# One core's hybrid decoder layer: state-space rooms laid out over attention's early heads, memory norm, constant rows and exp table first

## The chip, the cores and the metric

The kernel runs on one core of a Trainium2 chip. The metric is the device time of one execution in microseconds: the median of 3 runs before is 2584.89 us (2584.29 to 2587.09). The profile is of one execution; its span, from the first to the last instruction, is 2585.2 us.

The core has five engines that run side by side, each with a queue of its own that is worked off in order: TensorE (PE, matrix products; its weight loads are shown as PEld), VectorE (DVE), ScalarE (ACT), GpSimd (POOL) and SyncE (SP, which issues all DMAs of this kernel). On-chip memory (SBUF) has 128 partitions; rooms are told below in bytes of one partition. Products land in PSUM, 8 banks of 2 KB a partition.

## The reference

One layer over 1024 tokens of width 1024, in float32. Cut to what matters:

```
h = rms_norm(x, g_pre_mix)
q, k, v, z, xbc, dt_raw, ga, gs = split(h @ w_in)
o_att = stick_breaking_attention(q, k, v)          # 16 heads of 64, causal
o_ssm = ssd_branch(z, xbc, dt_raw, ...)            # 32 heads in 4 groups, chunks of 128
merged = sigmoid(ga) * (o_att @ w_br_att) + sigmoid(gs) * (o_ssm @ w_br_ssm)
x = x + rms_norm(merged @ w_mix_out, g_post_mix)
mem_n = rms_norm(mem, g_mem)                       # 256 memory tokens
x = x + rms_norm(cross_attention(rms_norm(x, g_pre_xa), mem_n, w_xq, w_xkv, w_xo), g_post_xa)
x = x + rms_norm(swiglu(rms_norm(x, g_pre_ffn), w_gu, w_down), g_post_ffn)
```

The output is compared in float32, so nearly every product is made of three: each operand is split into a high part, rounded to TensorE's faster format, and a low part (the difference), and high x high, high x low and low x high are added up.

## The kernel before

Stages follow each other: norm and v, z, the convolved part x|B|C and most gates (by a Winograd-like scheme with seven products for eight), then attention (from about 645 us), the state-space stage with the keys and values of the memory tokens (from 1091 us), the branch projections and the mix (from 1478 us), cross-attention (from 1661 us), and the feed-forward part.

**Order.** The code is written once, straight through. A scheduler then places the instructions on each engine's queue ahead of time, by a simulated timeline: earlier code has priority, but an instruction whose inputs and rooms are ready may go ahead of an earlier one that still waits. On the chip each queue is fixed. `behind(marks)` keeps instructions of an engine behind a given one on that engine; `issue_behind` does it for one instruction.

**Rooms.** Tiles live in pools. Left pools are stacked upward from the bottom of the memory, right pools downward from the top; a stage that closes its pools gives the place to the next. At the very bottom lie 16,384 bytes reserved as scratch for DMA descriptors that software writes. A tile laid over older tiles waits for the last reader of just those tiles (`reuse_waits="tile"`). Within a pool with several buffers of a tag, the program's layout gives out the lowest first, then the highest, then downward.

**Attention** (from L737) holds on the left the activations (hT, to byte 85,248; the second half of them, b22 and t1, is read by the last gate projections), and on the right, at the lower end, the pool `qk`: four rooms of 4,096 bytes each for the queries (qs, from 86,784), the high keys (kh, from 103,168) and the low keys (kl, from 119,552). Heads 12, 13, 14 and 15 have the first, fourth, third and second room of each; in order of time head 12 is done first, head 15 last. Above lie `wt` (wth and wtl, the turned attention weights, 135,936 to 152,320) and `beta` (n0, n1, the scans). For each head `scores` (L846) makes the score product (L858, L859), a sigmoid on ScalarE (L860) and a scan on VectorE (L861); `values` (L866) turns the result on PE (L875), copies it (L878), takes the difference (L879) and multiplies by v (L887, L888). The last four gate blocks (`gate_proj`, a sigmoid at L825) are strewn between the last heads as work for PE.

**The state-space stage** (from L948) opens with left pools over hT and qk and right pools `ots` and `w3` over beta, v and the projection weights. It first makes constants on GpSimd and VectorE: a triangle (`low`, L980), and the fixed part of the rows from which a chunk's decays are made (`colrows`, L993 and L994; `keyrows`, L996 and L997). `prep` (L1027) loads a chunk's rows, makes the decays by a product (L1048) and the exponent on ScalarE (L1049), and multiplies them (L1050). `states` and `outp` carry the state and make the output, `flip` turns it, `branch` projects it. Chunks of two ahead are prepared; 32 chunks in all.

Into this stage the memory tokens are woven. `memory(m)` (L1169) loads 128 token rows (L1171), takes the mean square on ScalarE (L1173), the root on GpSimd (`rstd_of`, L152 and L153), the norm on VectorE (L1174), turns them on PE (L1178) and stores high and low parts (L1180, L1181) in two 8 KB tiles of the pool `ots`. The gain g_mem is loaded into a weight room of `w3`. `mem_quanta` then makes keys and values from 16 weight blocks of 512 KB (load at L1194, split by L98 and L101), shared out evenly over the first eight steps of the chunk loop; from the second mark on each product is put behind the chunk's second-last marked product on PE's queue.

**Later rooms that the prediction speaks of:** `kT` (L1444), the keys for cross-attention, a right tile at 147,200 to 155,392; the gains `gx` (g_post_mix, g_pre_xa), a left pool at 146,688 to 154,880; the operand pool `opd` of the down projection, on the left from 118,016.

Of the kernel before, what the change touches and what calls it, by code (L numbers as in the profile page):

```python
# [34 lines left out]
def hybrid_block(ctx, tc, a, out, dbg=None):  # L35
# [213 lines left out]
    with ExitStack() as pa:  # L249
# [486 lines left out]
        with ExitStack() as p2:  # L736
# [14 lines left out]
            V.memset(mask, 0.0)  # L751
            G.affine_select(mask[:, S - P:], mask[:, S - P:], [[-1, P]], ALU.is_gt, 1.0, base=0, channel_multiplier=1)

            marks = []
            PIN = 8
            FQ = 1

# [88 lines left out]
            def scores(h, half, tb, ns_):  # L846
                def run():
                    hd = heads[h]
                    if half == 0 and tb == 0:
                        differences(h)  # L850
                    b = half * 4 + tb
                    L = (b + 1) * P
                    nt = mk(bp, [P, (half + 1) * HALF], F32, f"n{half}")
                    ns_.append(nt)
                    for s0 in range(0, L, HALF):
                        s1 = min(L, s0 + HALF)
                        ps = mk(psc, [P, HALF], F32, "sc")[:, :s1 - s0]
                        T.matmul(ps, hd["qs"][:, b * P:(b + 1) * P], hd["kh"][:, s0:s1], start=True, stop=False)  # L858
                        marks.append(T.matmul(ps, hd["qs"][:, b * P:(b + 1) * P], hd["kl"][:, s0:s1], start=False, stop=True))  # L859
                        A.activation(nt[:, s0:s1], ps, AF.Sigmoid, scale=-(HD ** -0.5))  # L860
# [68 lines left out]
            for m in range(NM):  # L929
                h, half = m // 2, m % 2  # L930
                hp, r = m // 4, m % 4
                s1 = [scores((m + 1) // 2, (m + 1) % 2, tb, ns_[m + 1]) for tb in range(4)] if m + 1 < NM else []
                if r == 3:
                    nxt = qk_quanta(hp + 2)
                dn = nxt[(r + 1) % 4]
                if m >= NM - 5:
                    n = -(-len(late) // (NM - m))
                    dn, late = late[:n], late[n:]
                interleave((values(h, half, ns_[m]), 0, 1), (s1, 0, 0.7), (dn, 0, 1))

    accp = pool(ctx, "a8", 4)
    acc_ = [mk(accp, [P, 2, S], F32, "a8") for _ in range(4)]
    acc = [acc_[f // 2][:, f % 2, :] for f in range(KT)]

# [1 line left out]
    p3b = ExitStack()  # L949
    with ExitStack() as p3:  # L950
        AHEAD = 2
        gb = pool(p3, "gbs", 2)
        sm = pool(p3, "smp", 2)
        t4 = pool(p3, "s4p", 3)
        t2 = pool(p3, "s2p", 9)
        ep = pool(p3, "exps", 1)
        wr = pool(p3, "wr3", 3)
        wp = pool(p3b, "w3", 2, side="right")
        ot = pool(p3b, "ots", 2, side="right")
        ps = pool(p3b, "ps3", 1, PSUM)  # L960
# [14 lines left out]

        NROW, HEADS, ONES, PAIRS, LARGE = 2, 32, 0, 64, 2.0 ** 127
        low = mk(ep, [P, P], F32, "low")
        G.memset(low, 1.0)  # L980
        G.affine_select(low, low, [[1, P]], ALU.is_ge, 0.0, base=0, channel_multiplier=-1)
        colrows = [mk(ep, [P, GH, P], F32R, f"colrows{i}") for i in range(NROW)]
        keyrows = [mk(ep, [P, HALF], F32R, f"keyrows{i}") for i in range(2)]
        before, within = mk(t4, [P, GH, P], F32, "s4"), mk(t4, [P, GH, P], F32, "s4")
        G.memset(before, 1.0)
# [95 lines left out]
        def outp(n):  # L1081
# [20 lines left out]
                    marks.append(ins)  # L1102
            V.tensor_tensor(y, y, pd, ALU.add)
            V.tensor_tensor(y, y, zs, ALU.mult)
            junk = mk(t2, [P, HALF], BF16, "junk", bufs=1)
            ms = mk(stats, [P, 1], F32, "ms")
            A.activation(junk, y, AF.Square, scale=float(HALF) ** -0.5, accum_out=ms)

# [19 lines left out]
        def halves():  # L1128

            return mk(wp, [P, 4, 2, HALF], F32R, "bw")  # L1130
# [28 lines left out]
                V.tensor_tensor(acc[f][:, sl], acc[f][:, sl], pb, ALU.add)  # L1159


        mh = mk(ot, [P, KT, ML], F32R, "oth")
        mlo = mk(ot, [P, KT, ML], F32R, "otl")
        gj = mk(wp, [P, 4, D], F32, "bw")
        gm, junk_m = gj[:, 0], gj[:, 1]
        nc.sync.dma_start(gm, a["g_mem"][0].partition_broadcast(P))
        marks = []

        def memory(m):  # L1169
            xt = mk(wr, [P, D], F32, "wraw")  # L1170
            nc.sync.dma_start(xt, a["mem"][0][m * P:(m + 1) * P, :])  # L1171
            ms = mk(stats, [P, 1], F32, "ms")
            A.activation(junk_m, xt, AF.Square, scale=D ** -0.5, accum_out=ms)  # L1173
            V.scalar_tensor_tensor(xt, xt, rstd_of(ms), gm, ALU.mult, ALU.mult)  # L1174
            for kh in range(2):
                pt = mk(ps, [P, 4, P], F32, "mm", bufs=2)
                for k in range(4):
                    T.transpose(pt[:, k, :], xt[:, (kh * 4 + k) * P:(kh * 4 + k + 1) * P], ident)  # L1178
                ks, cs = slice(kh * 4, kh * 4 + 4), slice(m * P, (m + 1) * P)
                A.activation(mh[:, ks, cs], pt, AF.Copy)  # L1180
                V.tensor_tensor(mlo[:, ks, cs], pt, mh[:, ks, cs].bitcast(F32), ALU.subtract)  # L1181

        def mem_quanta():

# [66 lines left out]

        for n in range(AHEAD):
            prep(n)
        for m in range(2):
            memory(m)
        mq = list(mem_quanta())
        NQ = len(mq)

# [610 lines left out]
```

## Time and profile before

| | us |
|---|---|
| median of 3 runs (lowest to highest) | 2584.89 (2584.29 to 2587.09) |
| span of the profiled execution (no other time is recorded for it) | 2585.2 |
| PE busy | 2493.1 |
| DVE busy | 1793.6 |
| ACT busy | 1130.1 |
| POOL busy | 842.2 |
| last score product of attention starts | 1070.20 |
| last product of attention's values starts | 1090.80 |
| products of the memory tokens, first starts | 1121.82 |

How to read it: the kernel's time is the span and a little around it. A busy PE includes the time that products take at a lower clock, so a window has to be read with the clock beside it (PEclk; 1.00 is full). A row of the timeline gives an instruction's start from the span's beginning, its length, and in brackets how long its engine stood idle before it and what released it. Products overlap: a 128x512 product at full clock is listed with 0.39 us, while the next one starts 0.23 us later.

### The profile page before, as it was taken

How to read it: one execution, taken by the hardware profiler on the slowest of the kernel's cores; microseconds unless marked ns; L12 is line 12 of the kernel's file. 1: busy time of each engine (PE TensorE's matmuls, PEld its weight loads, DVE VectorE, ACT ScalarE, POOL GpSimd, SP SyncE). 2: the span in 40 equal slices, each digit the busy share in tenths (PEclk: the TensorE clock that was granted, in tenths of full speed). 3: DMA queues.
4: the chain of work that ended last, by engine and by line, in shares of the span. 5: the costliest groups of instructions: out<-in, count | busy, mean ns of one | idle time of the engine just before them, and what ended most of it. 6: DMA issues, size and time to landing. Idle time of an engine off the chain costs nothing. (4 is left out here: it accounts for less than half of the span.)

```text
span 2585.2 us, 32334 instructions
## 1 busy us (share of the span) xinstructions
PE 2493.1 (96%) x11866; PEld 2061.1 (80%) x11866; DVE 1793.6 (69%) x2093; ACT 1130.1 (44%) x2020; POOL 842.2 (33%) x650
## 2 busy tenths in 40 slices
PE   7999999999999999999999999999999999999998
PEld 5788887887888778787888788887787888887876
DVE  7765777776578887687888664416459666666997
ACT  5333455555466655455554312314234333334343
POOL 3221654443111111244655050101114333323762
PEclk9999999999999999989999999999999999999999
DMA  7431433333543443355322462411232232224232
GB/s 245 155 121 58 151 117 103 109 106 91 141 107 98 118 104 90 111 180 175 104 90 81 153 238 74 130 49 50 94 113 70 76 96 74 90 90 163 98 131 98
DMA packets 255272, 293.44 MB, mean 114 GB/s; under 512 B 17024, under 2 KB 175241, under 8 KB 254987
## 3 DMA queue, kind: packets, MB, share of 16 engines
q1 hardware_dynamic: 255114, 291.40, 36.2%
q8 instruction: 93, 1.52, 0.2%
q14 instruction: 65, 0.52, 0.1%
HBM read 200.10 MB, written 74.45 MB: 106 GB/s over the span
## 5 line engine op out<-in xcount | busy, mean ns | idle before, releaser
L861 DVE TENSOR_TENSOR_SCAN n<-n,mask 128x128 f32<-128x128 f32 (+7 forms) x128 | 189.6, 1506 | 23.5 <-ACT n L860 22.2
L101 DVE TENSOR_TENSOR sw<-sf,sw 128x512 fp32r<-128x512 f32 x150 | 129.0, 872 | 67.0 <-ACT sw L98 66.7
L183 POOL TENSOR_TENSOR sf<-wr,wr 128x512 f32<-128x512 f32 x38 | 59.3, 1560 | 277.8 <-DMA wr<-in_w_gu_dram 138.3
L878 ACT ACTIVATE wth<-tr,mone 128x512 fp32r<-128x512 f32 x192 | 110.6, 584 | 83.0 <-PE tr L875 82.3
L98 ACT ACTIVATE sw<-sf 128x512 fp32r<-128x512 f32 x150 | 92.0, 626 | 109.1 <-PE mm L217 94.0
L879 DVE SCALAR_TENSOR_TENSOR wtl<-tr,wth 128x512 fp32r<-128x512 f32 x192 | 99.7, 544 | 50.6 <-ACT wth L878 50.6
L101 DVE TENSOR_TENSOR sw<-wr,sw 128x512 fp32r<-128x512 f32 x113 | 107.7, 955 | 27.6 <-ACT sw L98 27.5
L217 PE MATMUL mm<-h,sw 128*128 128x512 f32 x320 | 124.8, 391 | 1.8 <-DVE sw L101 1.8
L215 PE MATMUL mm<-h,sw 128*128 128x512 f32 x320 | 122.6, 391 | 2.9 <-ACT h L98 2.3
L216 PE MATMUL mm<-h,sw 128*128 128x512 f32 x320 | 125.1, 391 | 0.0
L104 PE MATMUL mm<-oth,bw 128*128 128x512 f32 (+1 forms) x320 | 122.5, 383 | 2.3 <-DVE a L1159 2.0
L98 ACT ACTIVATE sw<-wr 128x512 fp32r<-128x512 f32 x113 | 70.7, 628 | 120.9 <-PE mm L217 120.8
L106 PE MATMUL mm<-oth,bw 128*128 128x512 f32 (+1 forms) x320 | 120.0, 375 | 1.5 <-DVE bw L1146 1.5
L105 PE MATMUL mm<-otl,bw 128*128 128x512 f32 (+1 forms) x320 | 119.1, 372 | 0.0
L663 DVE SCALAR_TENSOR_TENSOR b<-b,prmT,b 128x1023 f32<-128x1023 f32 (+2 forms) x72 | 108.6, 1511 | 10.7 <-ACT b L661 10.0
L94 POOL TENSOR_SCALAR v<-va 128x512 fp32r<-128x512 f32 x16 | 20.6, 1291 | 285.4 <-PE av L888 165.8
L860 ACT ACTIVATE n<-sc 128x512 f32<-128x512 f32 (+1 forms) x192 | 88.6, 494 | 45.6 <-PE tr L875 28.8
L152 POOL TENSOR_SCALAR rstd<-ms 128x1 f32<-128x1 f32 x74 | 27.9, 376 | 242.3 <-ACT x L1380 111.5
L104 PE MATMUL p<-bw,h 128*128 128x512 f32 x256 | 99.4, 393 | 3.3 <-DVE x L1382 2.4
L106 PE MATMUL p<-bw,h 128*128 128x512 f32 x256 | 100.8, 394 | 0.0
L105 PE MATMUL p<-bw,h 128*128 128x512 f32 x256 | 100.4, 392 | 0.0
L185 POOL TENSOR_TENSOR sf<-wr 128x512 f32<-128x512 f32 x38 | 63.4, 1667 | 110.2 <-DVE sw L101 110.2
(607 smaller groups left out, 8033.1 us busy)
## 6 DMA issues: line engine op xcount, KB each, us to landing
wr<-in_w_gu_dram SPq DMA_DIRECT2D x80, 256.0 KB
wr<-in_w_in_dram SPq DMA_DIRECT2D x36, 512.0 KB
zr<-in_w_in_dram SPq DMA_DIRECT2D x28, 512.0 KB
gu_d<-t SPq DMA_DIRECT2D x44, 256.0 KB
wraw<-in_w_in_dram SPq DMA_DIRECT2D x20, 512.0 KB
zs_d<-zo SPq DMA_DIRECT2D x32, 256.0 KB
xs_d<-b SPq DMA_DIRECT2D x32, 256.0 KB
kl<-gt SPq DMA_DIRECT2D x64, 128.0 KB
```

The lines of the kernel that those rows point to most:

```text
L98: A.activation(o, i, AF.Copy)
L101: eng.tensor_tensor(o, i, hi.bitcast(F32), ALU.subtract)
L104: first = T.matmul(ps, sh, mh, start=start, stop=False)
L105: T.matmul(ps, sh, ml, start=False, stop=False)
L106: T.matmul(ps, sl, mh, start=False, stop=stop)
L215: T.matmul(ps, w[0][:, k, :], bh, start=first and k == 0, stop=False, skip_group_check=True)
L216: T.matmul(ps, w[0][:, k, :], bl, start=False, stop=False, skip_group_check=True)
L217: ins = T.matmul(ps, w[1][:, k, :], bh, start=False, stop=last and k == 3, skip_group_check=True)
L663: V.scalar_tensor_tensor(acc[:, sh:], y[:, :S - sh], cw(3 - sh, f), acc[:, sh:], ALU.mult, ALU.add)
L861: V.tensor_tensor_scan(nt[:, 0:L][:, ::-1], nt[:, 0:L][:, ::-1], mask[:, S - L:][:, ::-1], 1.0, ALU.mult, ALU.max)
L878: A.activation(wh[:, t0 * P:], pt[:, t0 * P:], AF.Identity, bias=mone)
L879: V.scalar_tensor_tensor(wl[:, t0 * P:], pt[:, t0 * P:], -1.0, wh[:, t0 * P:].bitcast(F32), ALU.add, ALU.subtract)
```

## The change

It touches the seam between attention and the state-space stage, and one line of the set-up.

- **Scratch.** The reserved bytes at the bottom go from 16,384 to 1,024. All left pools of the program sink by 15,360 bytes; right pools stay.
- **Exp table.** The sigmoids of the scores are collected (`sig`); behind the last one a one-column exp is put on ScalarE.
- **Memory tokens first.** `memory` is split in two: load and square (`memory_load`, both row tiles), then norm and turn (`memory`). Both stand ahead of the constants and of `prep` now, where before they stood behind `prep` of the first two chunks. The square's unused output goes into `mlo`; g_mem takes a raw room of the pool `wr3`.
- **Rooms.** The left pools of the stage are put in another order, and new ones are split off: `junk3` (the unused output of a chunk's square), `fill3` (512 bytes, never used), `memT` (mh and mlo, which were in `ots`) and `cols` (colrows; the pool `keys` keeps low and keyrows). A first weight room (`halves()`) and a first `dec` bank are taken and not used, so that those that follow come in the same turn as before.

| pool | before | after | what lay there in attention (after) |
|---|---|---|---|
| smp | 64,768 to 91,392 | 37,120 to 63,744 | activations (hT) |
| keys (low, keyrows) | in exps, 131,328 to 144,128 | 63,744 to 68,352 | activations |
| junk3, fill3 | in s2p; none | 68,352 to 69,888 | activations, to their end |
| memT (mh, mlo) | in ots, right | 69,888 to 86,272 | nothing |
| wr3 (raw blocks, token rows) | 144,128 to 156,416 | 86,272 to 98,560 | qs of heads 12, 15, 14 |
| s4p | 91,392 to 103,680 | 98,560 to 110,848 | qs of 14, 13; kh of 12, 15 |
| cols (colrows) | in exps | 110,848 to 119,040 | kh of 15, 14, 13 |
| s2p | 103,680 to 131,328 | 119,040 to 145,664 | kh of 13, kl, wth |
| gbs (states) | 52,480 to 64,768 | 145,664 to 157,952 | wtl, n0 |

The core of the diff:

```
-            marks = []
+            marks, sig = [], []
...
-                        A.activation(nt[:, s0:s1], ps, AF.Sigmoid, scale=-(HD ** -0.5))
+                        sig.append(A.activation(nt[:, s0:s1], ps, AF.Sigmoid, scale=-(HD ** -0.5)))
...
+            sig_last = sig[-1:]
...
+    with behind(sig_last):
+        A.activation(warm, mone, AF.Exp)
...
+        sm = pool(p3, "smp", 2)
+        ep = pool(p3, "keys", 1)
+        jk = pool(p3, "junk3", 1)
+        filler3 = pool(p3, "fill3", 1)
+        mk(filler3, [P, 128], F32, "fill3")
+        mtp = pool(p3, "memT", 1)
+        wr = pool(p3, "wr3", 3)
+        t4 = pool(p3, "s4p", 3)
+        cp3 = pool(p3, "cols", 1)
+        t2 = pool(p3, "s2p", 9)
         gb = pool(p3, "gbs", 2)
-        sm = pool(p3, "smp", 2)
-        t4 = pool(p3, "s4p", 3)
-        t2 = pool(p3, "s2p", 9)
-        ep = pool(p3, "exps", 1)
-        wr = pool(p3, "wr3", 3)
...
+        mh = mk(mtp, [P, KT, ML], F32R, "mh")
+        mlo = mk(mtp, [P, KT, ML], F32R, "mlo")
+        gm = mk(wr, [P, D], F32, "wraw")
+        nc.sync.dma_start(gm, a["g_mem"][0].partition_broadcast(P))
+        marks = []
+        mem_x = []
+        def memory_load(m):
+            xt = mk(wr, [P, D], F32, "wraw")
+            nc.sync.dma_start(xt, a["mem"][0][m * P:(m + 1) * P, :])
+            ms = mk(stats, [P, 1], F32, "ms")
+            A.activation(mlo.rearrange("p k t -> p (k t)")[:, m * D:(m + 1) * D], xt, AF.Square, scale=D ** -0.5, accum_out=ms)
+            mem_x.append((xt, rstd_of(ms)))
+        def memory(m):
+            xt, r = mem_x[m]
+            V.scalar_tensor_tensor(xt, xt, r, gm, ALU.mult, ALU.mult)
...
+        mk(ps, [P, 4, P], F32, "dec", bufs=2)
+        for fn in (memory_load, memory):
+            for m in range(2):
+                fn(m)
...
-        colrows = [mk(ep, [P, GH, P], F32R, f"colrows{i}") for i in range(NROW)]
+        colrows = [mk(cp3, [P, GH, P], F32R, f"colrows{i}") for i in range(NROW)]
...
-            junk = mk(t2, [P, HALF], BF16, "junk", bufs=1)
+            junk = mk(jk, [P, HALF], BF16, "junk")
...
-        mh = mk(ot, [P, KT, ML], F32R, "oth")
-        mlo = mk(ot, [P, KT, ML], F32R, "otl")
-        gj = mk(wp, [P, 4, D], F32, "bw")
-        gm, junk_m = gj[:, 0], gj[:, 1]
...
+        halves()
...
-        for m in range(2):
-            memory(m)
...
-    nc = _bacc.Bacc("TRN2", target_bir_lowering=False, num_devices=1)
+    nc = _bacc.Bacc("TRN2", target_bir_lowering=False, num_devices=1, dynamic_dma_scratch_size=1024)
```

More of the change, by code (lines that the diff above doesn't have):

```diff
@@ L970, in hybrid_block @@
         four = {}
+        mh = mk(mtp, [P, KT, ML], F32R, "mh")
[13 more added lines that the diff above has]
+            V.scalar_tensor_tensor(xt, xt, r, gm, ALU.mult, ALU.mult)
+            for kh in range(2):
+                pt = mk(ps, [P, 4, P], F32, "mm", bufs=2)
+                for k in range(4):
+                    T.transpose(pt[:, k, :], xt[:, (kh * 4 + k) * P:(kh * 4 + k + 1) * P], ident)
+                ks, cs = slice(kh * 4, kh * 4 + 4), slice(m * P, (m + 1) * P)
+                A.activation(mh[:, ks, cs], pt, AF.Copy)
+                V.tensor_tensor(mlo[:, ks, cs], pt, mh[:, ks, cs].bitcast(F32), ALU.subtract)
+        mk(ps, [P, 4, P], F32, "dec", bufs=2)
+        for fn in (memory_load, memory):
+            for m in range(2):
+                fn(m)
         NROW, HEADS, ONES, PAIRS, LARGE = 2, 32, 0, 64, 2.0 ** 127
@@ L1159, in branch @@
                 V.tensor_tensor(acc[f][:, sl], acc[f][:, sl], pb, ALU.add)
-        mh = mk(ot, [P, KT, ML], F32R, "oth")
-        mlo = mk(ot, [P, KT, ML], F32R, "otl")
-        gj = mk(wp, [P, 4, D], F32, "bw")
-        gm, junk_m = gj[:, 0], gj[:, 1]
[L1166 to L1181, printed above, removed]
+        halves()
         def mem_quanta():
```

## The prediction

> **What bounds the kernel now.** I read the cores first, then the busy tenths of the page, then the windows around the change.
>
> ```profile
> core 0: 2585.2 us, clock 0.990
> ...
> PE   7999999999999999999999999999999999999998
> ...
> DVE  7765777776578887687888664416459666666997
> ```
>
> One core works, and TensorE is busy in nearly every slice at full clock. So a change pays only where PE stands still, or runs at a lower clock, and later work can close up. The windows give the seam between attention and the state-space stage; columns are length, then busy time and count of PE, PEld, DVE, ACT and POOL, the granted clock, the DMA share and GB/s.
>
> ```profile
> 1051.00:1071.00 20.00, 20.00 (x101) 16.70 (x100) 9.70 (x12) 7.38 (x16) 0.00 (x0) 1.00 0.17 53
> 1071.00:1091.00 20.00, 17.89 (x100) 14.27 (x98) 12.25 (x18) 11.73 (x22) 11.03 (x12) 1.00 0.58 159
> 1091.00:1111.00 20.00, 15.18 (x68) 11.66 (x67) 19.47 (x23) 15.60 (x26) 11.13 (x9) 0.74 0.71 213
> 1111.00:1131.00 20.00, 16.99 (x93) 14.35 (x94) 18.26 (x23) 9.37 (x18) 7.62 (x9) 0.74 0.48 138
> 1131.00:1151.00 20.00, 20.00 (x169) 19.87 (x168) 12.22 (x14) 11.21 (x20) 7.20 (x7) 1.00 0.62 192
> ```
>
> From 1071 to 1131 PE loses 2.11 + 4.82 + 3.01 = 9.9 us idle, and (15.18 + 16.99) x 0.26 = 8.4 us to a clock of 0.74: 18.3 us, the ceiling of what this seam can return. Between 1091 and 1131 VectorE is the full engine (19.47 and 18.26 of 20), while it had 7.75 us free in the 20 us before. The timeline says why. These rows are start, length, engine, line, operation and, in brackets, idle time before and its releaser:
>
> ```profile
> 1070.20 0.39 PE L859 MATMUL sc<-kl,qs 128*128 128x512 f32 x1
> ...
> 1090.66 1.28 DVE L993 CAST colrows<-s 128x1024 fp32r<-128x1024 f32 x2
> ...
> 1090.80 0.33 PE L888 MATMUL av<-wtl,v 128*128 128x128 f32 x1
> ...
> 1091.60 0.38 SPq L1171 DMA_DIRECT2D wraw<-in_mem_dram  x1
> ...
> 1097.22 1.06 ACT L1173 ACTIVATE bw<-wraw 128x1024 f32<-128x1024 f32 x1 [0.28 <-DMA wraw<-in_mem_dram]
> 1098.19 0.19 ACT L1173 ACTIVATION_READ_ACCUMULATOR bw<-wraw 128x1 f32 x1
> ...
> 1098.39 0.43 SPq L1194 DMA_DIRECT2D wraw<-in_w_xkv_dram  x1
> ...
> 1098.77 1.30 POOL L153 TENSOR_TENSOR rstd<-rstd,mhalf 128x1 f32<-128x1 f32 x1
> ...
> 1103.71 1.05 ACT L98 ACTIVATE bw<-wraw 128x1024 fp32r<-128x1024 f32 x1
> ...
> 1120.67 1.27 DVE L1181 TENSOR_TENSOR otl<-mm,oth 128x512 fp32r<-128x512 f32 x2
> ...
> 1121.82 0.41 PE L104 MATMUL mm<-oth,bw 128*128 128x256 f32 x1
> ```
>
> The work that could fill PE, the products of the memory tokens, starts at 1121.82, right behind the last half of the turned tokens (otl). Its chain begins at 1091.60 with the load of the first token rows, because their room lies over attention's weight tiles (wtl), whose last reader is the product at 1090.80. The cast of the constant rows at 1090.66 stands behind the same rooms. Attention's last score product read its query and key rooms already at 1070.20.
>
> **The change part by part.** *Smaller scratch.* Left rooms sink by 15,360 bytes, right ones stay. Nothing is added, and no transfer needs the scratch: all data went by one hardware queue, and every issue row is SyncE's. Cost taken: nothing; its bound upward is a rival below.
>
> ```profile
> q1 hardware_dynamic: 255114, 291.40, 36.2%
> ```
>
> *Token rows, constant rows and their rooms.* The turned tokens (mh, mlo, 16 KB) now lie between the end of attention's activations and its lowest query room, free all through attention. The gain g_mem takes the lowest raw room, over head 12's queries, free long before. The two row tiles take the highest and the middle room; both touch head 15's queries (90,880 to 94,976, the higher one by 512 bytes), so they still wait for 1070.20. Their two loads pass ahead of the state-space loads on SyncE and move from 1091.60 to about 1071, 20 us. From there I use the same durations: 5.6 us to the square (1091.60 to 1097.22), 1.25 for it, 1.7 to GpSimd's end at 1100.07, 1.9 on VectorE (3.8 for two, below), 8 turns of PE, then copies and differences; the second tile two to three us behind. The last half stands at about 1087 instead of 1121.9. The first weight block has to wait, new in this version, for one of the three raw rooms (before, g_mem lay elsewhere): about 1083, plus 5.3 us (1098.39 to 1103.71), plus the split, 1.05 on ScalarE and 1.56 on VectorE (below): 1091. So the fill can begin about when attention ends, 30 us earlier.
>
> That is not 30 us of time, since VectorE is the full engine there. What leaves its full stretch is in the grouped lines (busy us, mean ns), all but the first of these rows, which is the difference of a weight block:
>
> ```profile
> L101 DVE TENSOR_TENSOR bw<-wraw,bw 128x1024 fp32r<-128x1024 f32 x4 | 6.2, 1561 | 1.7 <-ACT bw L98 1.7
> ...
> L1174 DVE SCALAR_TENSOR_TENSOR wraw<-wraw,rstd,bw 128x1024 f32<-128x1024 f32 x2 | 3.8, 1876 | 0.5 <-POOL rstd L153 0.5
> ...
> L1181 DVE TENSOR_TENSOR otl<-mm,oth 128x512 fp32r<-128x512 f32 x4 | 2.5, 676 | 0.0
> L994 DVE TENSOR_TENSOR colrows<-ident 16x1024 fp32r<-16x1024 f32 x2 | 2.3, 1211 | 0.0
> ...
> L993 DVE CAST colrows<-s 128x1024 fp32r<-128x1024 f32 x2 | 1.3, 683 | 0.0
> L997 DVE TENSOR_SCALAR keyrows<-low 2x512 fp32r<-2x512 f32 x2 | 0.8, 411 | 0.0
> L996 DVE CAST keyrows<-s 128x512 fp32r<-128x512 f32 x2 | 0.8, 419 | 0.0
> ```
>
> They are 11.5 us. The stretch 1071 to 1091 has 20 - 12.25 = 7.75 free, so 7.75 us are hidden there and 3.75 stay. The term lies between 0 (no step of the chain moves with it) and -18.3 (the ceiling); I take **-7.75**, since VectorE, being full, is the row nearest to the bound.
>
> *ScalarE.* To the same 20 us come two squares (2 x 1.25), four copies and the table work. The early exp is queued behind the last score sigmoid, which starts at 1070.63. But gate sigmoids follow; the first row below, of another view, has the copies (min, median and max ns):
>
> ```profile
> L1180 ACT ACTIVATE oth<-mm x4: 578/589/598, 1104.7 to 1113.8; 128x512 fp32r<-128x512 f32 x4
> ```
>
> ```profile
> 1070.63 0.60 ACT L860 ACTIVATE n<-sc 128x512 f32<-128x512 f32 x1 [1.67 <-PE sc L859]
> ...
> 1074.80 1.09 ACT L825 ACTIVATE gt<-mm 128x512 f32<-128x512 f32 x2 [1.19 <-PE mm L106]
> ...
> 1083.60 0.60 ACT L825 ACTIVATE gt<-mm 128x512 f32<-128x512 f32 x1 [0.24 <-PE mm L106]
> ...
> 1087.80 0.63 ACT L98 ACTIVATE ch<-cfm 128x512 fp32r<-128x512 f32 x1 [1.94 <-DMA cfm<-cf_d]
> ...
> 1098.39 1.28 ACT L1049 ACT_TABLE_LOAD   x1
> 1099.68 1.09 ACT L1049 ACTIVATE s<-dec 128x512 f32<-128x512 f32 x2
> ```
>
> So I expect three table loads where there is one: exp near 1071, sigmoid before 1074.80, exp again at the first chunk's exponent. The load that stood before the first exponent still stands there; two are added, 2 x 1.28 = 2.6 us. Together 2.5 + 2.4 + 2.6 = 7.5, against 20 - 11.73 = 8.3 free: hidden, barely. What is queued behind them is attention's weight copies (L878), for which DVE and then PE wait; without cover the cost is 2.6. I take 0. The Trainium skill, "ScalarE: Activation LUTs", section "What ACT_TABLE_LOAD costs", gives 1283 ns for the load and 1380 ns of drain at every switch. The trace agrees with the load; here the next activation starts 0.01 us after it, so no drain is to be seen. By the Trainium skill the two switches would be 5.3 us, which would not fit, and the sum would be 2.7 us higher.
>
> *Rooms elsewhere.* kT lay over the gain g_pre_xa, whose last reader is the VectorE instruction at 1668.15; in the new layout that gain is 15,360 bytes lower and kT's room is free.
>
> ```profile
> 1668.15 1.28 DVE L161 SCALAR_TENSOR_TENSOR x<-x,rstd,g_pre_xa 128x1024 f32<-128x1024 f32 x1 [0.98 <-POOL rstd L153]
> ...
> 1674.60 0.67 PE L1472 MATMUL p<-kT,qT 128*128 128x256 f32 x2 [0.67 <-DMA kT<-kT_d]
> ...
> 2357.27 0.50 PE L1645 MATMUL dnb<-op,op 128*128 128x512 f32 x1 [1.42 <-ACT op L98]
> ```
>
> PE waited 0.67 us for that load: **-0.67**. The start of the down projection (1.42 us of wait) also gets other rooms under its operands; it may lose this wait or get a like one: 0, bounds 1.42 both ways. The first attention-branch weights no longer wait for the square's scratch (its own room now), but PE has other products there: 0.
>
> Sum: -7.75 - 0.67 = -8.4; 2585.2 - 8.4 = 2576.8. The profiled span is 0.3 us over the median of the runs (2584.9), so 2576.5.
>
> **The rivals.**
>
> *The clock comes back too.* If PE has products from 1091 on, its clock need not fall, and part of the 8.4 us is saved on top: about 2568. For it speaks that the clock is 1.00 in all windows in which PE is full; against it that VectorE stays nearly full. The Trainium skill, "TensorE: Matmul & The Clock Gate", Part 1, says that the clock halves after an idle window of some 3.4 us and returns after as long a busy one. By that rule the 0.74 is a consequence of the gaps and goes with them.
>
> *The fill is spent, not added.* The memory products are a fixed supply, and each is queued behind a chunk's products. If the chunk steps do not move, the supply ends earlier than its last row now, and PE meets earlier what it meets in these windows:
>
> ```profile
> L104 PE MATMUL mm<-bw,oth x32: 388/393/507, 1151.7 to 1185.1; 128*128 128x512 f32 x32
> ...
> 1171.00:1191.00 20.00, 19.51 (x107) 16.24 (x106) 14.96 (x18) 11.02 (x20) 7.05 (x6) 1.00 0.62 192
> 1191.00:1211.00 20.00, 17.02 (x90) 13.64 (x89) 17.18 (x19) 13.41 (x26) 10.29 (x10) 1.00 0.64 220
> ```
>
> Without fill PE lost 2.98 us of 20 against 0.49 with it. Then most of the 7.75 is given back, some 1.5 us remain: 2583. Against it: the constant rows move too, and with them the first chunks.
>
> *Slower: ScalarE blocks attention's tail.* Its queue is in order. In the row at 1087.80 it stood 1.94 us for a load, with attention's copies behind it. Now the squares of both row tiles, loaded only from 1071 on, stand in that queue, each up to 5.6 us behind its load: 11.3 us at worst, and the two table loads 2.6: 13.9. Against the 8.4 gained that is +5.5: 2590.4. It decides from 8.4 us of such waits on. Against it: the loads overlap, and gate products keep PE busy until 1083.
>
> *It does not do what it says:* the exp table does not come first, which is in the sum already; and if the small scratch did bind transfers after all, DMA shares of 0.6 to 0.7 in the seam would rise and all stages would lose, which I give no more than 2 in 100, within the slower case.
>
> **How the numbers follow.** Forecast (2572 to 2579) 0.46, clock too 0.13, fill spent 0.24, slower 0.17. A measurement of this kernel tells about 0.2% (5.2 us) from no change: faster 0.46 + 0.13 = 0.59, the same 0.24, slower 0.17. The range goes from 2585 - 18.3 = 2567 to the slower case with one more wait of 1.42: 2592.
>
> **What would show it.** Right: token loads near 1071, last mlo near 1087, first memory product near 1091, constant rows cast before 1085; three table loads between 1070 and 1100; a clock above 0.74 in 1091 to 1131, and VectorE fuller before 1091. Wrong: ScalarE idle before a square with attention's copies late; attention's last product well after 1091; gaps after the memory products as long as those saved; a transition elsewhere (270, 645, 1480, 1960, 2357 us) shifted by more than 2 us.

## The result, and the profile after

The changed kernel took 2576.03 us (median of 4 runs, 2572.78 to 2577.68); the kernel before, beside it, 2585.02 (2584.29 to 2587.09). The ratio is 0.9961 with a 95% interval of 0.9949 to 0.9973: 7 to 13 us faster, against 8.4 forecast. The profiled span fell from 2585.2 to 2575.9. The total hides that one term was too large and two too small, so the stages come first.

Page and windows after; the columns of a window are length, busy time and count of PE, PEld, DVE, ACT and POOL, granted clock, DMA share and GB/s:

```profile
core 0: 2575.9 us, clock 0.993
...
1071.00:1091.00 20.00, 16.20 (x85) 12.25 (x84) 15.82 (x23) 13.56 (x25) 8.51 (x8) 0.98 0.56 182
1091.00:1111.00 20.00, 19.02 (x122) 17.39 (x123) 17.76 (x19) 14.49 (x25) 10.42 (x7) 0.85 0.71 225
1111.00:1131.00 20.00, 18.68 (x134) 16.79 (x133) 16.67 (x19) 9.82 (x17) 9.21 (x8) 1.00 0.61 173
1131.00:1151.00 20.00, 17.45 (x112) 15.02 (x111) 17.57 (x18) 13.12 (x24) 13.65 (x12) 1.00 0.66 207
1151.00:1171.00 20.00, 18.97 (x102) 15.92 (x101) 17.03 (x20) 12.42 (x22) 9.67 (x9) 1.00 0.56 186
1171.00:1191.00 20.00, 18.09 (x101) 15.03 (x99) 14.95 (x16) 11.74 (x21) 8.41 (x8) 1.00 0.61 205
1191.00:1211.00 20.00, 17.55 (x98) 14.32 (x97) 17.83 (x22) 11.90 (x24) 10.47 (x10) 1.00 0.44 134
1211.00:1231.00 20.00, 17.91 (x91) 15.30 (x90) 16.29 (x18) 9.55 (x21) 12.87 (x12) 0.91 0.34 95
```

Two windows of the kernel before that the prediction did not need:

```profile
1151.00:1171.00 20.00, 19.11 (x99) 15.54 (x97) 15.47 (x15) 10.87 (x19) 8.06 (x7) 1.00 0.54 185
1211.00:1231.00 20.00, 18.69 (x107) 16.07 (x106) 13.95 (x19) 11.30 (x22) 12.31 (x13) 1.00 0.29 88
```

Multiply PE's busy time by the clock to get its work. From 1091 to 1131 it was (15.18 + 16.99) x 0.74 = 23.8 us before and 19.02 x 0.85 + 18.68 = 34.8 after: 11.0 more, half of it filled idle time (5.5), half the clock. But from 1131 to 1231 the five windows fall from 94.3 to 88.4 (the last one at a clock of 0.91), 6.0 less, and from 1071 to 1091 from 17.9 to 15.9, 2.0 less. So some 3 us remain of 11, and another 0.9 comes after 1231. The gain stands where the change was made; what it cost stands in the windows on both sides.

Where PE stands can be read from first and last starts. The rows hold name, count, shortest, median and longest duration in ns, and the first and last start. Before:

```profile
L859 PE MATMUL sc<-kl,qs x192: 220/364/479, 670.8 to 1070.2; 128*128 128x512 f32 x96, 128*128 128x128 f32 x32, 128*128 128x256 f32 x32, 128*128 128x384 f32 x32
...
L888 PE MATMUL av<-wtl,v x192: 221/423/486, 685.7 to 1090.8; 128*128 128x512 f32 x96, 128*128 128x384 f32 x32, 128*128 128x256 f32 x32, 128*128 128x128 f32 x32
...
L105 PE MATMUL pst<-s2r,bh x28: 389/389/795, 1092.1 to 1413.0; 128*128 128x512 f32 x28
...
L104 PE MATMUL mm<-oh,whi x128: 389/389/500, 1478.3 to 1566.9; 128*128 128x512 f32 x128
...
L1472 PE MATMUL p<-kT,qT x128: 377/379/483, 1674.6 to 1785.5; 128*128 128x256 f32 x128
L1444 SPq DMA_DIRECT2D kT<-kT_d x1: 326/326/326, 1669.5 to 1669.5; - x1
...
L1645 PE MATMUL dnb<-fw,fg x24: 389/389/389, 2350.2 to 2369.2; 128*128 128x512 f32 x24
L1645 PE MATMUL dnb<-op,op x24: 389/389/504, 2357.3 to 2372.9; 128*128 128x512 f32 x24
```

And after:

```profile
L859 PE MATMUL sc<-kl,qs x192: 220/364/479, 670.1 to 1068.9; 128*128 128x512 f32 x96, 128*128 128x128 f32 x32, 128*128 128x256 f32 x32, 128*128 128x384 f32 x32
...
L888 PE MATMUL av<-wtl,v x192: 222/423/669, 684.9 to 1092.2; 128*128 128x512 f32 x96, 128*128 128x384 f32 x32, 128*128 128x256 f32 x32, 128*128 128x128 f32 x32
...
L105 PE MATMUL pst<-s2r,bh x28: 389/389/477, 1100.1 to 1407.7; 128*128 128x512 f32 x28
...
L104 PE MATMUL mm<-oh,whi x128: 389/389/500, 1472.5 to 1561.7; 128*128 128x512 f32 x128
...
L1490 PE MATMUL p<-kT,qT x128: 377/379/483, 1667.8 to 1779.5; 128*128 128x256 f32 x128
L1462 SPq DMA_DIRECT2D kT<-kT_d x1: 319/319/319, 1426.0 to 1426.0; - x1
...
L1663 PE MATMUL dnb<-fw,fg x24: 389/389/398, 2342.1 to 2359.4; 128*128 128x512 f32 x24
L1663 PE MATMUL dnb<-op,op x24: 389/389/395, 2347.6 to 2363.0; 128*128 128x512 f32 x24
```

From these come four lengths, in us. **Tail**: last score product to last product of values. **Chunks**: from there to the last state product (pst). **kT**: last product of the attention branch (oh) to the last one with kT. **Down**: first product of the down projection that uses the operands made before it (fw, fg) to the first that uses the loaded ones (op). The same rows, not rounded before subtracting, give the table for every kernel below; its names are those of the experiments:

```
                          tail   chunks  tail+chunks   kT     down
before                    20.6   322.2     342.8      218.7    7.0
after                     23.3   315.5     338.8      217.8    5.4
after, second profile     23.7   315.4     339.0      217.7    5.4
late rooms alone          19.9   321.4     341.3      217.7    5.4
late rooms back           23.7   317.2     341.0      218.5    6.9
order back                23.5   314.5     338.0      217.7    5.4
order alone               21.3   324.4     345.8      218.5    7.2
no early exp              23.7   315.1     338.8      217.7    5.4
splits behind the tail    20.5   314.3     334.8      217.7    5.4
both                      20.5   316.4     336.8      217.7    5.4
scratch, same rooms       20.7   322.1     342.8      218.5    7.1
lows on GpSimd            23.1   315.6     338.7      217.7    5.4
lows and splits           20.5   316.8     337.3      217.7    5.4
order back and splits     20.5   315.4     335.9      217.8    5.4
```

One profile of each: where the code up to there is the same, the chunks differ by up to 2 us between profiles (315.4 to 317.2), and kT and down, with the same rooms, by 0.1 to 0.3. With the late rooms as before these two stand at 218.5 to 218.7 and 6.9 to 7.2, with the sunk rooms at 217.7 to 217.8 and 5.4, without an exception.

### The profile page after: what moved, and what is told of

It is laid out like the page before. It is cut to its first block, busy times and chain, and to the rows that moved or that the text cites. A ratio compares the mean times of both kernels' runs of the same rounds, so it can differ in the third digit from the quotient of the medians.

```text
span 2575.9 us, 32333 instructions
## 1 busy us (share of the span) xinstructions
PE 2487.7 (97%) x11866; PEld 2057.5 (80%) x11866; DVE 1797.3 (70%) x2093; ACT 1132.1 (44%) x2023; POOL 852.9 (33%) x650
## 3 DMA queue, kind: packets, MB, share of 16 engines
q8 instruction: 93, 1.52, 0.2%
## 5 line engine op out<-in xcount | busy, mean ns | idle before, releaser
L878 ACT ACTIVATE wth<-tr,mone 128x512 fp32r<-128x512 f32 x192 | 110.6, 585 | 82.9 <-PE tr L875 81.0
L217 PE MATMUL mm<-h,sw 128*128 128x512 f32 x320 | 125.0, 392 | 1.8 <-DVE sw L101 1.8
L663 DVE SCALAR_TENSOR_TENSOR b<-b,prmT,b 128x1023 f32<-128x1023 f32 (+2 forms) x72 | 107.4, 1494 | 11.1 <-ACT b L661 10.4
L94 POOL TENSOR_SCALAR v<-va 128x512 fp32r<-128x512 f32 x16 | 20.6, 1288 | 283.8 <-PE av L888 166.0
L104 PE MATMUL mm<-oth,bw 128*128 128x512 f32 x256 | 103.6, 405 | 1.4 <-DVE a L1198 1.3
L106 PE MATMUL mm<-oth,bw 128*128 128x512 f32 x256 | 100.8, 394 | 0.1
L105 PE MATMUL mm<-otl,bw 128*128 128x512 f32 x256 | 100.5, 393 | 0.0
```

Source lines behind the costliest of these rows:

```text
L104: first = T.matmul(ps, sh, mh, start=start, stop=False)
L105: T.matmul(ps, sh, ml, start=False, stop=False)
L106: T.matmul(ps, sl, mh, start=False, stop=stop)
L217: ins = T.matmul(ps, w[1][:, k, :], bh, start=False, stop=last and k == 3, skip_group_check=True)
L663: V.scalar_tensor_tensor(acc[:, sh:], y[:, :S - sh], cw(3 - sh, f), acc[:, sh:], ALU.mult, ALU.add)
L878: A.activation(wh[:, t0 * P:], pt[:, t0 * P:], AF.Identity, bias=mone)
```

## The experiments

**The theory** after the comparison: the gain has two sources, the seam and the rooms of later stages, which sank by 15,360 bytes. The rival: all of it is the seam, and the later shifts are chance. All results below are ratios to the kernel before, run beside it on the same chip. The experiments ran on four chips, so kernels of different chips are compared by these ratios.

**1. Late rooms alone.** The kernel before, with

```diff
-    nc = _bacc.Bacc("TRN2", target_bir_lowering=False, num_devices=1)
+    nc = _bacc.Bacc("TRN2", target_bir_lowering=False, num_devices=1, dynamic_dma_scratch_size=1024)
...
         AHEAD = 2
+        early = pool(p3, "early", 1)
+        mk(early, [P, 15360 // 4], F32, "early")
```

> The kernel before, with the small scratch, and 15,360 bytes of filler opened ahead of the state-space stage's pools and given back behind them: that stage lies where it lay before, every left room after it lies 15,360 bytes lower, as in the changed kernel. Theory A (the gain has two sources, about half of it the seam and half the rooms of the later stages): 4 to 4.5 us faster than before, some 2580.5, with -3 us in cross-attention's stage (the first kT product against the last branch product) and -1.6 us at the start of the down projection, nothing between 1071 and 1480. Rival B (the whole gain is the seam, the later differences are chance of one profiled run): within 1.5 us of before, 2585.

Measured: 0.9978 (0.9966 to 0.9991), 2.3 to 8.8 us faster. kT 1.0 shorter, down 1.6 shorter, tail and chunks 1.5 shorter together, within their scatter. The rooms alone are worth time; the rival falls. The expected -3 us in cross-attention did not come: from the last product of the attention branch to the first with kT it was 1.6 shorter (107.7 to 106.1). Behind the last kT product the profile of before is long by chance: 564.7 us from there to the down projection, against 561.3 in experiment 4, which has the same rooms there. The load of kT shows the mechanism: it was issued at 1669.5 before, 5.1 us ahead of its first product; here

```profile
L1446 SPq DMA_DIRECT2D kT<-kT_d x1: 320/320/320, 1431.7 to 1431.7; - x1
```

**2. Late rooms back.** The changed kernel, with

```diff
+    filler("fill_late", 15360)
     x1 = ExitStack()
     with ExitStack() as p4:
```

> The changed kernel, with 15,360 bytes of filler opened on the left behind the state-space stage: the seam is that of the changed kernel, all later left rooms lie where they lay before. Theory A: 3.5 to 4.5 us slower than the changed kernel (2576.0), some 2580: the seam's gain of 4.6 us stays, the later one goes, and the first kT product waits 0.67 us again. Rival B: 2576, as the changed kernel.

Measured: 0.9993 (0.9985 to 1.0002), 1.8 us faster than before (from 0.5 slower to 3.9 faster). So more of the changed kernel's gain is gone than the 3.5 to 4.5 expected; by stage, kT and down are back to 218.5 and 6.9, and the seam keeps 1.8. The load of kT is late again, and the down projection waits again. Rows of one tile, then of PE's waits (in all, times, longest):

```profile
L1463 SPq DMA_DIRECT2D kT<-kT_d x1: 327/327/327, 1666.5 to 1666.5; - x1
```

```profile
PE dnb L1664 <- ACT op L98: 1.3, 1, 1.3
```

That wait is the 1.42 us that the prediction left open. Before, one of the first loaded tiles (op) lay over a room of the up projection's results (t), and its split waited for a store of them:

```profile
2336.26 14.14 SPq L1550 DMA_DIRECT2D gu_d<-t  x2
...
2356.17 1.06 ACT L98 ACTIVATE op<-wr 128x1024 fp32r<-128x1024 f32 x1 [6.62 <-DMA gu_d<-t]
```

After, both splits run together, long before they are needed:

```profile
2340.40 2.00 ACT L98 ACTIVATE op<-wr 128x1024 fp32r<-128x1024 f32 x2
```

**3. Order back.** The changed kernel with the memory tokens written again behind `prep` of the first two chunks:

```diff
-        gm = mk(wr, [P, D], F32, "wraw")
-        nc.sync.dma_start(gm, a["g_mem"][0].partition_broadcast(P))
...
-        for fn in (memory_load, memory):
-            for m in range(2):
-                fn(m)
...
         for n in range(AHEAD):
             prep(n)
+        gm = mk(wr, [P, D], F32, "wraw")
+        nc.sync.dma_start(gm, a["g_mem"][0].partition_broadcast(P))
+        for fn in (memory_load, memory):
+            for m in range(2):
+                fn(m)
```

> The changed kernel, but the gain, the two row tiles and their turns are written again behind the constant rows and the first two chunks, as before; rooms, scratch and early exp are those of the changed kernel. Theory A1 (the rooms make the seam's gain: constant rows and token loads are free 20 us earlier in any order): the token loads pass behind the state-space loads, a few us later than 1069, and the time is within 1.5 us of the changed kernel, 2576 to 2577.5. Rival A2 (the order makes it): the memory tokens' chain stands behind two chunks on VectorE, as before, and 3 to 4.6 us are lost: 2579 to 2580.6.

Measured: 0.9975 (0.9966 to 0.9985), by which 2585.0 us become 2578.6: between the two forecasts. Tail and chunks are 338.0, the shortest of all kernels with this tail, but from the last state product to the last product of the attention branch this profile took 157.0 us, the two of the changed kernel 154.0 and 155.8. So up to the last state product the order of writing costs nothing here; the time alone does not decide, and experiment 12 asks again. One expectation failed: the token loads did not pass behind the state-space loads. They are issued at 1066.02, 0.4 us behind the last score product, just as in the changed kernel (1069.31 behind 1068.9). With the rooms free, the scheduler put the loads, squares and norms where they were, whatever the order of writing.

**4. Order alone.** The kernel before, its rooms and scratch, with the changed order and the early exp:

```diff
+        mh = mk(ot, [P, KT, ML], F32R, "oth")
+        mlo = mk(ot, [P, KT, ML], F32R, "otl")
+        gj = mk(wp, [P, 4, D], F32, "bw")
...
+        for fn in (memory_load, memory):
+            for m in range(2):
+                fn(m)
...
         for n in range(AHEAD):
             prep(n)
-        for m in range(2):
-            memory(m)
```

> The kernel before, with its rooms and its scratch, but with the gain, the row tiles, their turns and the early exp in the order of the changed kernel. Theory A1 (rooms): the row tiles still wait for attention's weight tiles, to about 1091, and stand on SyncE ahead of the state-space loads, so that the chunks start later: 0 to 3 us slower than before, 2585 to 2588, first memory product after 1110. Rival A2 (order): 3 to 4.6 us faster than before, 2580.4 to 2582.

Measured: 1.0011 (1.0001 to 1.0022), 0.3 to 5.7 us slower; tail and chunks 345.8, 3.0 longer than before. Both token loads, at 1089.23 and 1090.85, stand ahead of the loads into the constant rows, and the first memory product starts at 1120.6, as A1 has it. Together with 3: the rooms make the seam's gain, the order without them only puts late loads ahead of useful ones.

**5. The changed kernel again**, as the base of the three runs after it.

> The changed kernel once more, as the base of the runs beside it on the same chip, and for a second profile. Theory A (seam and later rooms): 8 to 10 us faster than before; by stage, attention's tail (last score product to last product of values) 2.5 to 3 us longer than before, the state-space stage about 6 us shorter, the first kT product 1 us nearer and the start of the down projection 1.7 us nearer. Rival B (only the first pair of profiles showed the later gains): tail and state-space stage as above, but 218.7 to the last kT product and 23.0 to the down projection, as before, and 4 to 5 us faster in all.

Measured: 0.9955 (0.9941 to 0.9969). Its tail, chunks, kT and down are those of the first profile within 0.4, so rival B falls. The tail is 3.1 longer than before. Its timeline in the first profile of after shows what stands there:

```profile
1069.31 0.81 SPq L996 DMA_DIRECT2D wraw<-in_mem_dram  x2
...
1069.93 1.28 ACT L947 ACT_TABLE_LOAD   x1
...
1072.99 1.28 ACT L825 ACT_TABLE_LOAD   x1
...
1075.25 1.06 ACT L998 ACTIVATE mlo<-wraw 128x1024 fp32r<-128x1024 f32 x1
...
1080.44 1.28 DVE L1003 SCALAR_TENSOR_TENSOR wraw<-wraw,rstd,wraw 128x1024 f32<-128x1024 f32 x1 [0.58 <-POOL rstd L153]
...
1082.38 0.66 PE L875 MATMUL tr<-ident,n 128*128 128x128 f32 x4 [0.49 <-DVE wtl L879]
...
1089.00 0.63 ACT L98 ACTIVATE ch<-cfm 128x512 fp32r<-128x512 f32 x1 [2.75 <-DMA cfm<-cf_d]
...
1090.15 0.69 PE L887 MATMUL av<-wth,v 128*128 128x384 f32 x1 [2.21 <-ACT wth L878]
...
1092.46 1.93 PE L1007 MATMUL mm<-ident,wraw 128*128 128x128 f32 x8
...
1095.95 1.28 ACT L1088 ACT_TABLE_LOAD   x1
...
1100.63 0.28 PE L104 MATMUL mm<-mh,bw 128*128 128x256 f32 x1
...
1103.86 0.68 DVE L1010 TENSOR_TENSOR mlo<-mm,mh 128x512 fp32r<-128x512 f32 x1
```

ScalarE stands 2.75 us for a load of the next stage, while attention's weight copies, which PE needs, are queued behind that split. The same split waited before the change too, 1.94 us (the prediction's row at 1087.80), and PE behind it:

```profile
1088.95 0.45 PE L887 MATMUL av<-wth,v 128*128 128x384 f32 x1 [1.64 <-ACT wth L878]
```

Two things could have made the tail longer: the two added table loads (theory C), or a longer wait here (theory D).

**6. No early exp.**

```diff
-    with behind(sig_last):
-        A.activation(warm, mone, AF.Exp)
```

> The changed kernel without the early exp: one table load, at the first exponent, in place of three. Theory C (the two added loads lengthen attention's tail, since the copy of the turned weights stands behind them on ScalarE): tail 1.3 to 2 us shorter than in the changed kernel (23.3), and 1 to 2 us faster in all. Rival D (the tail is longer because the first split of the state-space stage waits on ScalarE for its load, with the weight copies behind it): tail unchanged, 23 to 23.5, and the time within 0.7 us.

Measured: 0.9953 (0.9940 to 0.9967), tail 23.7. There is one table load left, and nothing is gained: C falls. PE's wait, first in the second profile of after, then here, is the same:

```profile
PE av L887 <- ACT wth L878: 2.6, 1, 2.6
PE tr L875 <- DVE wtl L879: 1.3, 3, 0.5
```

```profile
PE av L887 <- ACT wth L878: 2.6, 1, 2.6
PE tr L875 <- DVE wtl L879: 1.2, 2, 0.7
```

**7. The two splits behind the tail.** `wts` collects the copies of the turned weights (L878):

```diff
-            hi_sb(bh, btm, "a")
+            with behind(wts_last if (g, q) == (0, 0) else []):
+                hi_sb(bh, btm, "a")
...
-            hi_sb(ch, cfm, "a")
+            with behind(wts_last if (g, q) == (0, 0) else []):
+                hi_sb(ch, cfm, "a")
```

> The changed kernel, with ScalarE's first two splits of the state-space stage (bh and ch of the first four chunks) put behind attention's last copy of turned weights. Theory D (the wait of that split for its load holds attention's tail): PE's wait of 2.2 us ahead of the last three products of values goes, the tail is 2 us shorter, some 21.3, and the kernel 1.5 to 2 us faster than the changed one. Theory C: at most 0.5 us, since the weight copies are late for another reason.

Measured: 0.9951 (0.9936 to 0.9967). The wait of 2.6 is gone and the tail is 20.5 us, 3.2 shorter, as D has it:

```profile
PE mm L1008 <- DVE mlo L1011: 3.6, 1, 3.6
PE tr L875 <- DVE wtl L879: 1.0, 2, 0.5
```

```profile
L859 PE MATMUL sc<-kl,qs x192: 220/364/479, 665.9 to 1065.5; 128*128 128x512 f32 x96, 128*128 128x128 f32 x32, 128*128 128x256 f32 x32, 128*128 128x384 f32 x32
...
L888 PE MATMUL av<-wtl,v x192: 221/422/486, 680.7 to 1086.0; 128*128 128x512 f32 x96, 128*128 128x384 f32 x32, 128*128 128x256 f32 x32, 128*128 128x128 f32 x32
```

Here PE waits 3.6 us at the second set of turns instead, behind VectorE's low parts, and still tail and chunks are 4 us shorter. The time, 2571.62 against 2572.56 for the changed kernel beside it, does not tell the two apart; 1.5 to 2 us were expected.

**8. Both edits.**

> The changed kernel with both edits: no early exp, and the two splits behind attention's last weight copy. If C and D add: tail 19.5 to 20.5 us, 3 to 4 us faster than the changed kernel. If what the tail gives back is lost again in the state-space stage, where VectorE is busy for 16 to 18 us of every 20: within 1 us of the changed kernel.

Measured: 0.9948 (0.9934 to 0.9963), tail 20.5, chunks 316.4. The tail is that of 7: the table loads cost nothing there even when that wait does not cover them. The median, 2571.85, is 0.7 us under that of the changed kernel beside it, so C and D do not add; that the chunks are 2 us longer than in 7 (316.4 against 314.3) is within their scatter.

**9. Scratch with the same rooms.** The kernel before with the small scratch and

```diff
-FILL_LEFT, FILL_RIGHT = 96, 224
+FILL_LEFT, FILL_RIGHT = 96 + 15360, 224
```

> The kernel before with the small scratch, and 15,360 bytes of filler at the left end for the whole program: every room but those of the constants and small sums lies where it lay before. Theory E (the scratch itself is worth nothing, as predicted; what the stages don't explain is the scatter of single executions): within 1.5 us of before, and 23.0 us from the last product of the up projection's input to the down projection, as before. Rival F (the scratch itself gives the 3 to 5 us by which the times fell more than the stages add up to): 2581 to 2582, 3 us or more under before.

Measured: 1.0001 (0.9988 to 1.0013), at most 3.4 us either way. The scratch itself is worth nothing that can be measured; the effect that shows is where the rooms lie.

**10. Half of the memory blocks' low parts on GpSimd**, on the changed kernel, to test the prediction's premise that VectorE is what the seam waits for:

```diff
-                lo_of(lo, raw, hi)
+                lo_of(lo, raw, hi, G if i else V)
```

> The changed kernel, with every second difference of the memory weight blocks (8 of 16, 1.56 us each on VectorE) on GpSimd instead. Theory G (in the stretch in which the memory products are made VectorE is what the chunk steps wait for): about 12.5 us of VectorE's work go, the state-space stage (315.5 us) gets 2 to 5 us shorter, and the kernel as much faster than the changed one. Rival H (the steps wait for a chain through all engines, and GpSimd, over 10 us busy of 20 there, is the slower place): stage within 1 us or up to 3 us longer.

Measured: 0.9964 (0.9951 to 0.9978); chunks 315.6. Eight differences left VectorE and the stage did not move, as H says. But G is not refuted by it, because VectorE hardly got emptier. Lines of 1090 to 1240 (count, then busy us and mean ns), first of the changed kernel, then of this one:

```profile
L101 DVE TENSOR_TENSOR bw<-wraw,bw 128x1024 fp32r<-128x1024 f32 x16 | 24.2, 1516 | 6.3 <-ACT bw L98 6.3
L101 DVE TENSOR_TENSOR s2r<-s,s2r 128x512 fp32r<-128x512 f32 x14 | 12.6, 899 | 4.8 <-ACT s2r L98 4.7
```

```profile
L101 DVE TENSOR_TENSOR s2r<-s,s2r 128x512 fp32r<-128x512 f32 x14 | 15.2, 1087 | 6.8 <-ACT s2r L98 6.5
L101 DVE TENSOR_TENSOR bw<-wraw,bw 128x1024 fp32r<-128x1024 f32 x8 | 13.1, 1632 | 4.0 <-ACT bw L98 4.0
...
L101 POOL TENSOR_TENSOR bw<-wraw,bw 128x1024 fp32r<-128x1024 f32 x8 | 22.4, 2800 | 0.0
```

The moved differences took 11.1 us off VectorE, but other instructions, no more of them than before, got longer: the difference of s by 2.6 us here, the product of s and cb by 3.1 (20.6 to 23.7). In the 150 us behind attention's last product VectorE was busy for 125.0 us, against 127.3 to 129.6 in experiment 6 and the two profiles of the changed kernel; GpSimd for 105.6, against 81.2 to 82.2. And VectorE's waits for a GpSimd sum (L1134) rose from 1.2 to 4.7.

**11. The same on top of 7.**

> The kernel with the two splits behind attention's last weight copy, and with half of the memory blocks' differences on GpSimd. Tail 20.5 us as there, and the state-space stage as G or H have it: under G 2 to 5 us shorter than 314.3, in all 5 to 8 us faster than the changed kernel; under H 3 us faster at most.

Measured: 0.9951 (0.9932 to 0.9970), tail 20.5, chunks 316.8. The times are those of H again, and the run leaves the same doubt.

**12. Order back and splits.**

> The changed kernel's rooms with the old order (memory tokens behind the first two chunks), and the two splits behind attention's last weight copy. Theory A1 (rooms decide, the order of writing doesn't): tail 20.5 us and state-space stage 314 to 316 us, as with the new order and the same splits (20.5 and 314.3), and 3 us shorter by stage than the changed kernel (23.3 to 23.7 and 315.5). Rival A2 (the order is worth 3 us or more once the tail no longer hides it): stage 317 us or longer.

Measured: 0.9942 (0.9928 to 0.9956), the lowest ratio of all; tail 20.5, chunks 315.4, as A1 has it. Tail and chunks, 335.9, lie among those of the three kernels with the new order and the same splits (334.8 to 337.3), so the order of writing costs nothing that shows. By stage it is 3 us ahead of the changed kernel; by time its interval overlaps with that of the changed kernel (0.9941 to 0.9969).

## Why the prediction was right, point by point

**The total** was right (2576.5 against 2576.03), by terms that were off in both directions, and with a rest that was traced to no term. That it agrees to half a microsecond is luck. (One reading in it was wrong without consequence: an execution's time is some 1.8 us over its own span, 2577.68 against 2575.9 in the profiled one after, so the span of 2585.2 fits the longest of the three executions before, 2587.09, and not the median. The difference of 8.4 is the same from either.)

**The seam, -7.75.** It measured -4.0 in the first pair of profiles, and -2.7 as a mean of the three profiles with the seam of before (342.8, 341.3, 342.8) and the three with that of after (338.8, 339.0, 341.0). The term that was too large is "7.75 us are hidden there". VectorE's busy time in 1071 to 1091 rose from 12.25 to 15.82 us, by 3.6 and not by 7.75 (by 3.3, counted in both from 0.8 us behind the last score product); the low parts of the turned tokens were to be hidden there too, and they came behind attention. And work put beside attention's tail is not free, because the tail is on PE's path too. The chunks gained 6.7 in the first pair, near the figure, but the tail lost 2.7. PE makes the same 102 products in both tails. Its idle time there went from 2.1 to 3.8 us: 0.6 is the longer wait for the weight copy (2.21 against 1.64), and 1.0 the two waits for VectorE's low parts (0.49 and 0.47, at 1082.38 and 1086.47, which before does not have). The other 1.0 is in the products, which took 19.5 us in place of 18.5; the one behind the wait, for example, 0.69 against 0.45. Experiment 7 takes the split's wait away and with it 3.2 us of the tail; tail and chunks of the four kernels with this edit are 5.5 to 8.0 under before.

**VectorE as the bound.** The premise that chose -7.75 between 0 and -18.3 is neither shown nor refuted. Experiments 10 and 11 were made to test it, but of the 11 us moved only 2 to 5 left VectorE's busy time. PE's waits between 1131 and 1231, where it lost 10 us idle, end with VectorE for 5.8 us and with ScalarE for 4.1, none longer than 2.2, so VectorE is not the only engine that the chunks wait for. That their -6.7 came near -7.75 does not speak for the premise, since only 3.6 us had been hidden.

**The chain's times.** Loads at 1069.31, constant rows cast before 1085 and the second norm at 1080.44 came as forecast. The turns did not: their inputs were there by 1081.7, yet they start at 1092.46, without a wait in brackets, since they are placed behind attention's last product in PE's fixed order: the step "8 turns of PE" had left that queue out. So the first memory product came at 1100.63 and the last low part at 1103.86, not at 1091 and 1087.

**The rivals "clock" and "fill spent"** were weighed as alternatives; both happened in one run. The clock in 1091 to 1131 went from 0.74 to 0.85 and 1.00, worth 5.5 us, and from 1131 on the windows gave 6.0 back. That was one of the prediction's own signs of being wrong (gaps behind the memory products as long as those saved), and it came with a total that was right.

**ScalarE, 0.** Three table loads, at 1069.93, 1072.99 and 1095.95, and no cost: right, by 6 and 8. The slower rival ("ScalarE blocks attention's tail") named the right queue and the wrong instruction: not the squares and the table loads, but the first chunk's split, which waits for its load. Without this wait the tail is some 3 us shorter; but it stood there before the change too, and the change made PE's part of it only 0.6 us longer, not 13.9, so it did not decide.

**kT, -0.67.** Right in cause. Behind the attention branch the first product came 1.7 earlier (107.7 to 106.0), the last 0.9.

**Down projection, 0 within 1.42.** It came out at its good end, and a little past it: -1.6, the wait gone.

**The scratch itself, 0:** right, by 9.

**What stays open.** The terms found add up to -2.7 - 0.9 - 1.6 = -5.2 (-6.5 with the seam of the first pair), while the two timings of the changed kernel say -7 to -13 and -8 to -15. Experiments 1 and 2 together make -5.7 and -1.8. The rest, some 4 to 6 us from the middle of the intervals (10.1 and 11.6) and 0.5 to 2 from the near end of the first, was not traced to a place. The first low score product of attention starts between 665.9 and 671.4 us over all these profiles in no order that a layout explains (670.1 and 666.9 in the two of the changed kernel). From the last kT product to the down projection it is 560.7 to 564.7 in the four profiles with the late rooms of before and 559.4 to 562.6 in the others, too much overlap to claim it. What holds the chunks between 1131 and 1231 stays open as well.

## What to carry to other kernels

A change of a reserved size moves every room behind it: look through the whole program for tiles that lie over a late reader or a late store, and price each wait on its own, at both ends. Work that is moved ahead of a stage's end stands in the same in-order queues as that end: before counting it as hidden, look for an instruction that waits for a load there, with the end's own work behind it. And where one engine is nearly full, take a little work off it in an experiment before taking it as the bound, and read in the trace whether it did get emptier.

## What the runs showed of the hardware

Two added table loads of 1.28 us on ScalarE cost nothing measurable, next to a split that waits 2.75 us for a load and also without it. GpSimd made the difference of a 128x1024 block in 2.80 us on average (experiment 10), VectorE in 1.52 (the changed kernel).

VectorE's times went with what GpSimd did beside it. In the 150 us behind attention's last product of the changed kernel's first profile, the 128x512 difference s2r, which reads two tiles in SBUF, took 0.68 us on average in the six cases in which GpSimd was idle, and 1.12 in the six in which GpSimd was busy for more than half of its length; in experiment 10 it was 0.69 (four) and 1.34 (eight). The sum of state and pst, which reads one of its two inputs from PSUM, took 0.68 us in both cases, in both kernels. Why is not shown here.

Executions of the kernel before scattered from 2575.2 to 2590.5 us on one chip (23 executions), while the stretch from the attention branch to the last kT product repeated to 0.1 us in the ten profiles with sunk rooms (217.7 to 217.8).
